# Decode values on column tiles with a norm per sequence, and every channel tile of the convolution as Toeplitz products on 32x32 array tiles

## The chip, the core and the metric

The kernel runs on one core of one Trainium2 chip. The metric is the device time of one execution in microseconds; the time before is 1244.36 us (median of three runs, 1243.08 to 1247.17).

Engines are named as in the profile: PE is TensorE's matmul side and PEld its weight loads, DVE is VectorE, ACT ScalarE, POOL GpSimd, SP the engine that issues most of the DMAs (POOL issues the others).

## The reference

One inference step through two layers, for a prompt of 1024 frames and for 8 running sequences of 16 new frames (1152 tokens together, width 1024). Everything is float32. What matters for the change, shortened:

```python
# layer 0, a running sequence: 1024 cached keys and values and 16 new ones, 4 heads, two maps c
s = einsum('bqhcd,bkhcd->bhcqk', q, k) * 64 ** -0.5 + bias
p = softmax(s)
w = p[:, :, 0] - lam * p[:, :, 1]
o = einsum('bhqk,bkhe->bqhe', w, v)
o = rmsnorm(o, subln_g) * 0.8                    # over the 128 values of a head
out_a = o * silu(g_a)

# layer 1: gated input, depthwise convolution of width 31 over time, LayerNorm over channels
a, b, g = split(rmsnorm(x) @ w_in1, 3)
u = a * sigmoid(b)
ctx = concat([conv_state, u])                    # 30 earlier rows (zeros for the prompt)
c = depthwise_conv(ctx, w_dw) + b_dw             # 1024 channels, each with its own 31 taps
c = silu(layernorm(c)) * silu(g)
y = x + c @ w_out1
```

## The kernel before

Four stages follow each other on the core: the projections of layer 0, the prompt's attention and gating, decode together with layer 0's output projection, and layer 1. Most products are split by hand into a high and a low part in the type fp32r and done as three products (mm3, L155: high times high, low times high, high times low). split_w loads a weight block into one of three raw buffers, ACT casts the high part (L143) and DVE subtracts for the low one (L144). Plain F32 products are also used; the profile shows each of these as two matmul instructions.

The framework orders each engine's instructions by its own estimate of their times and by priorities; each engine then works through its list in order. A DMA waits in the list of the engine that issues it, and what stands behind it waits too.

**Decode.** For each of the 8 sequences, dscores makes scores of 32 rows per head (two maps of 16 queries), the four heads on four column tiles of the array (L730, tiles KT and S), and their exponentials ex. dweights folds the two maps with the matrix cf into transposed weights of 64 columns (4 heads of 16) for 9 key tiles: 8 of the cache and one of the new tokens (L758), and writes them as high and low parts into wt (L761, L762). dvalues loads V in four chunks of 512 KB through two buffers (vraw, L772, issued by POOL), splits each on ACT and DVE (vh L775, vl L776), and makes, for each of the 9 key tiles, two products over all 512 columns (L783, L784, and L784, L786 for the new tokens' tile vs). Only the blocks where a query's head meets that head's columns are wanted, so DVE multiplies by a mask (om, L788), and one F32 product with a placing matrix (L790) puts the 16 rows in their place among 128, where DVE adds them up in oacc (L794). After the last sequence dfinish takes the norms of all sequences and multiplies by the gate. Between these stand prep and main, the output projection of the prompt's token tiles, whose weights are loaded in the first two sequences.

**Layer 1.** conv_tile runs once for each of 8 channel tiles: six groups of 24 products (L155), two for each of three token chunks (b, then a), the sigmoid on ACT (sb, L1103), and u as their product on DVE. Five of the tiles (0, 1, 3, 5, 7) are convolved on DVE by 31 taps for the prompt (L1148, 1024 columns) and 31 for the sequences (L1146). Three (PE_TILES = 2, 4, 6) are convolved on PE: u goes to DRAM (s_u) and comes back as X, with 16 channels by 8 time steps on the partitions; POOL builds block matrices tw from the turned filters (L1166); 5 F32 products of 128x128 for each of 8 groups sum to the result (L1172); ACT copies it to Y (L1173); it goes to DRAM (s_c) and comes back as yb, and ACT adds the bias into cT (L1180, L1183). The four steps of a Toeplitz tile stand behind the third to sixth product groups of the next channel tile (hooks TOEP). msum (L952, POOL) adds up the channel tiles for the LayerNorm. Then come 24 groups of gate products with their SiLU on ACT (sg, L1021), three norm_chunk calls behind gate tiles 4, 5 and 6, and the last projection, whose first weights are loaded after the gates. Products and gates of layer 1 share a PSUM pool (pm2) of three buffers.

## Time and profile before

| | us |
|---|---|
| median of three runs | 1244.36 |
| the profiled execution | 1244.07 |
| its span, first to last instruction | 1242.3 |
| PE busy in the span | 1163.6 |
| DVE busy in the span | 807.9 |
| decode's first scores | 512.25 |
| layer 1's first products | 755.5 |
| the last gate products | 1128 |

The mean granted clock of the span is 0.975. Times within the span count from its start. A PE instruction's duration reaches from its start to its modelled end, and neighbours overlap: what a product costs in a dense row is the distance to the next one's start.

### The profile page before, as it was taken

What the parts mean: (1) busy time and instruction counts of PE and PEld (TensorE: products, weight loads), DVE (VectorE), ACT (ScalarE), POOL (GpSimd) and SP (SyncE); (2) the same over time, 40 slices, a digit from 0 to 9 for tenths busy, and PEclk for the clock granted to TensorE, in tenths of its full rate; (3) what the DMA queues carried; (4) which work ended last, traced back from release to release, by engine and by line L of the source; (5) the groups of instructions that cost most, each with busy time, mean ns of one, the idle gap of its engine ahead of it and who ended that gap; (6) DMA issues with size and microseconds to landing.
All of it is one profiled execution on the core that took longest, in us unless ns stands there. A gap on an engine that the chain in (4) does not pass through costs nothing.

```text
span 1242.3 us, 18215 instructions
## 1 busy us (share of the span) xinstructions
PE 1163.6 (94%) x6516; PEld 1038.4 (84%) x6516; DVE 807.9 (65%) x1663; ACT 461.0 (37%) x1058; POOL 364.3 (29%) x516
## 2 busy tenths in 40 slices
PE   6999999999989997779999998999999987998997
PEld 4878998999989987557776767999999987997886
DVE  5420225688787778765555444899989999267843
ACT  4431223545454545554435334111121212256421
POOL 2232223344354335322322220112424220033300
PEclk9999999999989998889999999999999998999999
DMA  8352444414141314877766646113321310212231
GB/s 298 107 157 73 148 145 136 126 55 120 41 122 46 103 49 137 287 246 238 238 220 237 194 145 174 45 41 89 97 85 60 112 60 24 68 35 102 80 124 68
DMA packets 122042, 153.23 MB, mean 123 GB/s; under 512 B 13697, under 2 KB 85401, under 8 KB 121944
## 3 DMA queue, kind: packets, MB, share of 16 engines
q1 hardware_dynamic: 107968, 108.21, 28.1%
q0 software_dynamic: 13840, 43.60, 10.5%
q8 instruction: 52, 0.85, 0.3%
q14 instruction: 38, 0.31, 0.1%
q10 hardware_dynamic: 144, 0.26, 0.1%
HBM read 116.22 MB, written 36.26 MB: 123 GB/s over the span
## 4 chain that ended last, share of the span: by engine, by line
PE 75%; DMA 9%; DVE 6%; issue 5%; ACT 3%; POOL 1%; SPq 0%; DVEq 0%; POOLq 0%; ACTq 0%
PE mm L155 51%; PE out L155 7%; PE py L1172 3%; PE pa L587 2%; PE tr L416 2%; DMA vraw<-in_cache_v 1%; PE tr L165 1%; PE S L544 1%; PE mm L784 1%; PE S L545 1%; PE mm L783 1%; PE tr L582 1%; DMA big<-s_c 1%; DMA s_c<-big 1%; PE S L730 1%
## 5 line engine op out<-in xcount | busy, mean ns | idle before, releaser
L155 PE MATMUL mm<-yh,wh 128*128 128x384 f32 x576 | 196.4, 341 | 15.2 <-ACT sg L1021 12.7
L155 PE MATMUL mm<-yh,wl 128*128 128x384 f32 x576 | 195.4, 340 | 0.2 <-DVE wl L144 0.2
L155 PE MATMUL mm<-yl,wh 128*128 128x384 f32 x576 | 195.4, 339 | 0.0
L155 PE MATMUL mm<-wh,xh 128*128 128x384 f32 (+1 forms) x504 | 185.4, 369 | 1.5 <-DVE sg L467 0.6
L1148 DVE SCALAR_TENSOR_TENSOR acc<-u,cc,acc 128x1024 f32<-128x1024 f32 x145 | 185.7, 1281 | 0.4
L155 PE MATMUL mm<-wl,xh 128*128 128x384 f32 (+1 forms) x504 | 184.3, 366 | 1.5 <-DVE wl L144 1.5
L155 PE MATMUL mm<-wh,xl 128*128 128x384 f32 (+1 forms) x504 | 183.5, 364 | 0.0
L144 DVE TENSOR_TENSOR wl<-raw,wh 128x1024 fp32r<-128x1024 f32 (+1 forms) x72 | 91.3, 1275 | 91.8 <-ACT wh L143 88.4
L155 PEld LDWEIGHTS mm<-yh,wh 128*128 128x128 f32 x576 | 109.2, 190 | 16.0 <-ACT sg L1021 13.0
L155 PEld LDWEIGHTS mm<-yh,wl 128*128 128x128 f32 x576 | 109.1, 190 | 0.6 <-DVE wl L144 0.5
L155 PEld LDWEIGHTS mm<-yl,wh 128*128 128x128 f32 x576 | 109.2, 190 | 0.3
L155 PEld LDWEIGHTS mm<-wh,xh 128*128 128x128 f32 x504 | 95.7, 190 | 13.1 <-issue 1.1
L155 PEld LDWEIGHTS mm<-wl,xh 128*128 128x128 f32 x504 | 95.6, 190 | 11.4 <-DVE wl L144 2.9
L155 PEld LDWEIGHTS mm<-wh,xl 128*128 128x128 f32 x504 | 95.5, 189 | 8.8 <-DVE xl L168 0.3
L143 ACT CAST wh<-raw 128x1024 fp32r<-128x1024 f32 (+1 forms) x72 | 71.4, 1001 | 70.0 <-PE mm L155 32.2
L124 POOL TENSOR_TENSOR rr<-pw,mhalf 128x1 f32<-128x1 f32 x59 | 38.4, 651 | 165.9 <-DVE pw L123 157.4
L558 ACT ACTIVATE e<-S,nm 128x512 f32<-128x512 f32 (+5 forms) x96 | 55.0, 578 | 53.7 <-DVE nm L553 36.2
L155 PE MATMUL out<-wh,ch 128*128 128x512 f32 x144 | 59.9, 416 | 1.7 <-DVE xr L844 1.2
L1166 POOL TENSOR_TENSOR tw<-wx,same 128x640 f32<-128x640 f32 x24 | 37.3, 1558 | 82.3 <-PE py L1172 72.5
L550 DVE TENSOR_REDUCE nm<-S 128x1 f32<-128x512 f32 (+5 forms) x96 | 52.5, 551 | 10.5 <-PE S L545 9.7
L155 PE MATMUL out<-wh,cl 128*128 128x512 f32 x144 | 58.8, 408 | 0.0
L155 PE MATMUL mm<-wl,ch 128*128 128x512 f32 x144 | 56.4, 392 | 2.3 <-DVE wl L144 2.2
(282 smaller groups left out, 2400.0 us busy)
## 6 DMA issues: line engine op xcount, KB each, us to landing
raw<-in_cache_k SPq DMA_DIRECT2D x32, 512.0 KB, 4.4
vraw<-in_cache_v POOLq DMA_DIRECT2D x32, 512.0 KB, 5.4
raw<-in_w_in SPq DMA_DIRECT2D x24, 512.0 KB, 5.1
raw<-in_w_out SPq DMA_DIRECT2D x16, 512.0 KB, 4.6
raw<-in_w_in SPq DMA_DIRECT2D x32, 256.0 KB, 3.4
raw<-in_w_in SPq DMA_DIRECT2D x48, 128.0 KB, 3.1
s_y<-xr POOLq DMA_DIRECT2D x9, 512.0 KB, 4.7
x<-s_y SPq DMA_DIRECT2D x9, 512.0 KB, 4.2
```

Source lines behind the costliest of these rows:

```text
L124: m = nc.gpsimd.tensor_tensor(out, v[:, :w], self.mhalf[:, :w], ALU.pow)
L143: nc.scalar.copy(h[:, :ks * n], raw[:, :ks * n])
L144: (low or nc.vector).tensor_tensor(l[:, :ks * n], raw[:, :ks * n], h[:, :ks * n].bitcast(F32), ALU.subtract)
L155: m = self.nc.tensor.matmul(out, lhsT=x, rhs=y, start=(i == 0), stop=(i == n - 1))
L165: nc.tensor.transpose(ps[:, k * P:(k + 1) * P], src[:, kk * P:(kk + 1) * P], self.ident)
L416: nc.tensor.transpose(ps[:, h * P:(h + 1) * P], src[:, h * P:(h + 1) * P], self.ident)
L550: nc.vector.tensor_reduce(nm[:, j:j + 1], s[:, :n], AX.X, ALU.max, negate=True)
L558: nc.scalar.activation(e[:, j * n:(j + 1) * n], S[j][:, :n], AF.Exp, bias=nv, accum_out=zz[:, j:j + 1])
L587: nc.tensor.matmul(po, lhsT=wT[:, k * P:(k + 1) * P], rhs=hd["v"][:, k, :], start=(k == 0), stop=(k == qb))
L1148: tap = nc.vector.scalar_tensor_tensor(cv[:, :T] if k == CONV - 1 else acc, u[:, k:k + T], w1, acc, ALU.mult, ALU.add)
L1166: nc.gpsimd.tensor_tensor(tw.rearrange("p s (c f) -> p s c f", f=8), wx[:, g, :].rearrange("p (s f) -> p s f", f=8).unsqueeze(2).broadcast ...
L1172: nc.tensor.matmul(py, lhsT=tw[:, 4 - s, :], rhs=X[:, g, s:s + 176], start=(s == 0), stop=(s == 4))
```

## The change

**Decode.** V is no longer split: the products are plain F32. Each of the 9 key tiles gives four products, one per head, with 16 weight columns and the head's 128 value columns, on the four column tiles; the wanted blocks alone come out, in one 128x128 block of PSUM (pvt). Mask, placing product, oacc and the split of wt are gone. The norm, with the gate, is done per sequence, and the rows are stored for sequences 0 to 6 together and for the last one. V has five buffers (VB), and vload fetches it one sequence ahead. The scores and value products are issued with a raised priority (HPS).

**Layer 1.** All eight channel tiles take the Toeplitz path. The products are 32x32: 4 channels by 8 time steps on each of four row strips. A tile has two steps of 80 products, behind the fourth and fifth group of the next channel tile. Four PSUM banks take the results, rotated over the partitions, and the store to s_c undoes the rotation in seven DMAs. The bias is a step of its own (back), on DVE, behind the first product u of the tile after next. The last two of these stand in the first gate tiles, whose sg buffers are now held from the start. norm_chunk stands behind gate tiles 3, 4 and 5, and the first half of the output weights is loaded from gate tile 4 on.

```diff
-PE_TILES = (2, 4, 6)
+HPS = 300
+VB = 5
-TOEP = (2, 3, 4, 5)
+TOEP = (3, 4)
+HPT = 400
-LN_AT = (4, 5, 6)
+LN_AT = (3, 4, 5)
...
+        def vload(b):
+            if b >= NB:
+                return
+            cv = a["cache_v0"][b].rearrange("(t p) h e -> p t (h e)", p=P)
+            seqs[b]["V"] = []
+            for i in range(4):
+                vr = vp.tile([P, 1024], F32, name="vraw", bufs=VB).rearrange("p (t c) -> p t c", t=2)
+                nc.gpsimd.dma_start(out=vr, in_=cv[:, 2 * i:2 * i + 2])
+                seqs[b]["V"] += [vr[:, 0], vr[:, 1]]
+            seqs[b]["V"].append(vs)
...
         def dvalues(b):
+            wt, V = seqs[b]["wt"], seqs[b]["V"]
+            pav = pvt[:, b % 2 * P:(b % 2 + 1) * P]
+            with tc.high_priority(offset=HPS):
+                for k in range(8, -1, -1):
+                    for h in range(H):
+                        nc.tensor.matmul(pav[h * 32:h * 32 + NQ], lhsT=wt[:, k, h * NQ:(h + 1) * NQ],
+                                         rhs=V[k][:, h * P:(h + 1) * P], start=(k == 8), stop=(k == 0))
             jk = ep.tile([P, P], F32, name="jk", bufs=1)
+            ss = self.small.tile([P, 1], F32, name="ss")
+            nc.scalar.activation(jk, pav, AF.Square, accum_out=ss)
+            rm = self.small.tile([P, 1], F32, name="rr")
             self.rpow(rm, ss, 1.0 / P, 1e-6)
+            nc.vector.scalar_tensor_tensor(og[:, b], pav, rm, gs[:, b], ALU.mult, ALU.mult)
...
             if b > 0:
                 dvalues(b - 1)
+                vload(b)
...
         dvalues(NB - 1)
         prep(6)
-        dfinish()
...
+            for i in range(8):
...
+                late = (lambda j=i - 2: back(j)) if i > 1 else None
+                tiles.append(self.conv_tile(i, wb, pm, ub, cT[i], chan, (s_u, s_c), same, hooks_of(i), late))
...
+            if c == 0 and late is not None:
+                with tc.issue_after(mu.ins if hasattr(mu, "ins") else mu):
+                    late()
...
         def step(q):
+            tw = ub.tile([P, 20, 32], F32, name="tw", bufs=2)
+            nc.gpsimd.tensor_tensor(
+                tw.rearrange("p s (c f) -> p s c f", f=8),
+                wx[:, 4 * q:4 * q + 4].rearrange("p g (s f) -> p (g s) f", f=8).unsqueeze(2).broadcast_to([P, 20, 4, 8]),
+                same.rearrange("p (c f) -> p c f", f=8).unsqueeze(1).broadcast_to([P, 20, 4, 8]), ALU.mult)
+            with tc.high_priority(offset=HPT):
                 for s in range(5):
+                    for j in range(4):
+                        for r in range(4):
+                            rs, c = slice(r * 32, (r + 1) * 32), (r + j) % 4
+                            nc.tensor.matmul(self.py[j][c * 32:(c + 1) * 32, q * 256:q * 256 + 176],
+                                             lhsT=tw[rs, j * 5 + 4 - s, :], rhs=X[rs, 4 * q + j, s:s + 176],
+                                             start=(s == 0), stop=(s == 4))
+            for j in range(4):
+                nc.scalar.copy(Y[:, 4 * q + j, :], self.py[j][:, q * 256:q * 256 + 176])
+            if q == 0:
+                return
+            sv = s_c[i].rearrange("(g p) m -> p g m", p=P)
+            for j in range(4):
+                k = j * 32
+                nc.sync.dma_start(out=sv[:P - k, j::4], in_=Y[k:, j::4])
+                if j:
+                    nc.sync.dma_start(out=sv[P - k:, j::4], in_=Y[:k, j::4])
+            yb = ub.tile([P, 8, 176], F32, name="big", bufs=4)
+            nc.sync.dma_start(out=yb, in_=s_c[i].rearrange("(p f) m -> p f m", f=8))
...
+        def back():
+            yb, bia = ret["yb"], chan[:, i, 0:1]
+            nc.vector.tensor_scalar(cv[:, :T].rearrange("p (m f) -> p m f", f=8),
+                                    yb[:, :, :P].rearrange("p f m -> p m f"), bia, None, ALU.add)
```

Three places in the built order show what moved. Rows give the line, the operation and output<-inputs with the output's rows and columns; a count at the end joins like rows. The changed program's line numbers are its own.

PE at the first value products of decode, before:

```order
L758 MATMUL mm<-cf,ex 128x64 x9
L416 MATMUL tr<-cst_58,raw 128x128 x8
L783 MATMUL mm<-vh,wt 128x512
L784 MATMUL mm<-vl,wt 64x512
L783 MATMUL mm<-vh,wt 128x512
L784 MATMUL mm<-vl,wt 64x512
```

and now, at the same place (L759 is the weights, L414 the key transposes, L782 the values, pv the new PSUM block):

```order
L759 MATMUL mm<-cf,ex 128x64 x8
L759 MATMUL pv<-cf,ex 128x64
L414 MATMUL tr<-cst_58,raw 128x128 x8
L782 MATMUL pv<-vs,wt 16x128 x4
L782 MATMUL pv<-vraw,wt 16x128 x32
```

The 18 products over 512 columns became 36 products of 16x128, which read V as it was loaded and stand in one piece.

PE at the first Toeplitz step of a channel tile, now (py_8250 to py_8253 are the four banks; the row behind is a projection). Before, a step had two rows of five products with 128 rows, L1172, with projections between them:

```order
L1140 MATMUL py_8250<-big,tw 32x176 x4
L1140 MATMUL py_8251<-big,tw 32x176 x4
L1140 MATMUL py_8252<-big,tw 32x176 x4
L1140 MATMUL py_8253<-big,tw 32x176 x4
L1140 MATMUL py_8250<-big,tw 32x176 x4
```

Each row of four holds the four row strips of one bank, and the sixteen products of four rows share no array tile; five such blocks are a step.

ACT at the first gate, before (L1173 copies Toeplitz results, L1180 and L1183 add the bias, L1021 is the gates' SiLU):

```order
L1173 COPY big<-py 128x176 x2
L1180 ACTIVATE cT_8260<-big,cc 128x1024
L1183 ACTIVATE cT_8260<-big,cc 128x8x8 x2
L1021 ACT_TABLE_LOAD
L1021 ACTIVATE sg_10366<-mm 128x384 x3
```

and now (L1144 copies Toeplitz results, L146 casts weights, L958 is the SiLU):

```order
L1144 COPY big<-py_8253 128x176
L146 CAST wh<-raw 128x1024 x2
L958 ACT_TABLE_LOAD
L958 ACTIVATE sg_8268<-mm 128x384 x2
```

No addition of a bias stands ahead of the first SiLU any more; it is on DVE.

More of the change, by code (lines that the diff above doesn't have):

```diff
@@ L796, in dfinish @@
-        def dfinish():
-            ss = self.small.tile([P, H], F32, name="ss4")
+            wt = ep.tile([P, 9, 64], F32, name="wt", bufs=2)
+            ps = pm.tile([P, 512], F32, name="mm")
+            p8 = pvt[:, 256 + b % 2 * 64:320 + b % 2 * 64]
+            for k in range(9):
+                nc.tensor.matmul(ps[:, k * 64:(k + 1) * 64] if k < 8 else p8, lhsT=ex[:, k, :], rhs=cf,
+                                 start=True, stop=True)
+            nc.scalar.copy(wt[:, :8], ps.rearrange("p (k e) -> p k e", e=64))
@@ new lines, in phase_conv @@
+            chan = cp.tile([P, 8, 4], F32, name="cc")
+            same = cp.tile([P, 32], F32, name="same")
+            nc.sync.dma_start(out=chan, in_=self.s_cc.rearrange("p (i n) -> p i n", n=4))
+            nc.sync.dma_start(out=same, in_=a["cst"][:, C_SAME:C_SAME + 32])
+            s_u = self.dram.tile([8, P * 8, 180], F32, name="s_u")
+            s_c = self.dram.tile([8, P * 8, 176], F32, name="s_c")
+            s3 = E(ExitStack())
+            ubs = ExitStack()
+            ub = ubs.enter_context(tc.tile_pool(name="ub", bufs=2, reuse_waits="tile"))
@@ new lines, in phase_conv, with back, hooks_of @@
+            tiles = []
+            def back(i):
+                tiles[i][2]()
+                if i == 1:
+                    nc.gpsimd.tensor_tensor(msum, cT[0], cT[1], ALU.add)
+                elif 1 < i < 7:
+                    nc.gpsimd.tensor_tensor(msum, msum, cT[i], ALU.add)
+            def hooks_of(i):
+                hooks = {}
+                if i > 0:
+                    hooks[TAIL] = [tiles[i - 1][0]]
+                    for p, f in zip(TOEP, tiles[i - 1][1]):
+                        hooks.setdefault(p, []).append(f)
+                return hooks
@@ L969, in phase_conv @@
+            for i in range(2):
+                if i == 0:
+                    wb = self.split_w(wp, [a["w_in1"][:, 2 * D:2 * D + 256]], 256)
+                gate_tile(i, wb)
+                if i == 0:
+                    back(6)
+            back(7)
+            ubs.close()
             pl.close()
@@ L1091, in hook @@
             nonlocal npc
-            with self.tc.issue_after(m):
+            with tc.issue_after(m):
                 for f in hooks.get(npc, ()):
@@ L1189 @@
+        return tail, [lambda q=q: step(q) for q in range(2)], back
 _INS = ["x_prompt", "x_sample", "cache_k0", "cache_v0", "state_conv1", "rel_bias", "norm_g0", "w_in0",
```

290 lines of the change are left out of this document (87 added, 203 removed).

## The prediction

> **What bounds the kernel now.** I read the page's busy shares, its slices and its chain first.
>
> ```profile
> PE 1163.6 (94%) x6516; PEld 1038.4 (84%) x6516; DVE 807.9 (65%) x1663; ACT 461.0 (37%) x1058; POOL 364.3 (29%) x516
> ...
> PE   6999999999989997779999998999999987998997
> ...
> DVE  5420225688787778765555444899989999267843
> ...
> PE 75%; DMA 9%; DVE 6%; issue 5%; ACT 3%; POOL 1%; SPq 0%; DVEq 0%; POOLq 0%; ACTq 0%
> ```
>
> TensorE is busy nearly everywhere and carries 75% of the chain. VectorE is full only in slices 25 to 34, the convolution. So work taken from VectorE is worth only what TensorE waits for it, and work taken from TensorE counts where nothing else sets the pace. The stages differ, so I cut the span into decode, convolution with gates, and the last projection; columns are the stretch, then busy us and count for PE, weight loads, DVE, ACT, POOL, then granted clock, DMA share, GB/s.
>
> ```profile
> 512.25:755.50 243.25, 224.06 (x1305) 166.19 (x1304) 131.88 (x221) 107.75 (x207) 65.56 (x88) 0.96 0.66 219
> 755.50:1128.00 372.50, 352.88 (x2060) 348.73 (x2059) 305.67 (x421) 91.79 (x169) 91.76 (x84) 0.98 0.24 73
> 1128.00:1242.30 114.30, 103.53 (x455) 83.70 (x453) 69.45 (x160) 44.89 (x125) 20.72 (x16) 0.98 0.27 97
> ```
>
> The change touches the first two rows: 616 us. A PE busy time includes the tail of each product, so below I use the distance between starts instead.
>
> **Decode values.** The old value products, three groups of the lines view, and single rows of the timeline:
>
> ```profile
> L783 PE MATMUL mm<-vh,wt 128*128 128x512 f32 x64 | 28.2, 440 | 5.2 <-DVE wt L762 5.2
> L790 PE MATMUL mm<-om,mk 128*128 128x512 f32 x16 | 8.3, 598 | 0.0
> ...
> 706.08 0.40 PE L783 MATMUL mm<-vh,wt 128*128 128x512 f32 x1
> 706.31 0.40 PE L784 MATMUL mm<-vl,wt 128*64 128x512 f32 x1
> ...
> 512.25 1.50 PE L730 MATMUL S<-KT,qz 128*32 128x256 f32 x24
> ...
> 684.10 0.39 PE L783 MATMUL mm<-vh,wt 128*128 128x512 f32 x1
> 684.42 0.67 PE L730 MATMUL S<-KTx,qz 128*32 128x272 f32 x8
> 685.01 0.44 PE L165 MATMUL tr<-cst,raw 128*128 128x128 f32 x2
> ```
>
> A sequence has 9 key tiles, each with a high and a low product: 18 starts 0.23 us apart (706.08, 706.31) are 4.1 us, and the placing product adds 8.3/8 = 1.0. Eight sequences: 41 us. The new products have not run, but their like has: L730 puts the four heads on four column tiles. An F32 product is two passes, so its 24 instructions are 6 groups of four; 1.50 us less one product's 0.38 (the rest of a tail) leaves 5 steps of 0.22 us. Four of 256 columns thus cost what one would: the column tiles do run side by side. With 128 columns a group costs 0.11, and 9 tiles in two passes make 18 groups: 2.0 us. Entering and leaving the tiling costs about 0.1 us each way (684.10 to 684.42 is 0.32 where 0.23 is usual; 684.42 to 685.01 is 0.59 for two groups of 0.25). So 2.2 us a sequence, 17.6 in all: TensorE is relieved of 23.8 us. ACT's and DVE's splits of V go as well; they matter only through the next rows.
>
> How much arrives? The chain of waits inside decode, with start and length of its pieces, and two windows:
>
> ```profile
> 646.07 5.49 PE out L155 x24
> ...
> 657.04 2.59 DVE vl L776
> ...
> 659.92 8.15 DMA vraw<-in_cache_v
> ...
> 699.02 6.08 PE out L155 x19
> ...
> 540.00:550.00 10.00, 8.59 (x69) 5.69 (x67) 8.33 (x12) 6.14 (x9) 3.73 (x5) 1.00 1.00 355
> 600.00:627.00 27.00, 27.00 (x169) 19.97 (x169) 15.26 (x26) 12.59 (x25) 8.98 (x13) 1.00 0.76 233
> ```
>
> The same piece returns after two sequences, so a period is 52.95/2 = 26.5 us. It goes through the V load: a load (8.15) starts only once the low split has freed one of two buffers (657.04). The new five buffers, filled a sequence ahead, cut that link. What is late next is TensorE or the DMA engines: they move 6.3 MB a period at a share of 0.76, and 26.5 less 2.8 would put them at 0.85, below the 1.00 and 355 GB/s that they reach elsewhere. In the first two sequences the loads of keys, V and output weights set the pace (share 1.00 in 540 to 550), so there I count nothing. I take six periods of 2.8: **-17 us**. Ends: 0 (the loads take it all) and -41 (all 23.8, and some 2 us a period of present waiting as well).
>
> **The wait ahead of the gates.** PE and ACT rows of the timeline; brackets give the wait and who ended it.
>
> ```profile
> 1018.58 0.33 PE L155 MATMUL mm<-yl,wh 128*128 128x384 f32 x1
> 1018.75 0.34 PE L155 MATMUL mm<-yh,wl 128*128 128x384 f32 x1
> 1018.93 1.68 PE L1172 MATMUL py<-big,tw 128*128 128x176 f32 x10
> 1033.32 0.69 PE L155 MATMUL mm<-yh,wh 128*128 128x384 f32 x1 [12.71 <-ACT sg L1021]
> 1033.80 0.52 PE L155 MATMUL mm<-yl,wh 128*128 128x384 f32 x1
> 1034.12 0.52 PE L155 MATMUL mm<-yh,wl 128*128 128x384 f32 x1
> ...
> 1028.84 2.03 ACT L1180 ACTIVATE cT<-big,cc 128x1024 f32<-128x1024 f32 x1 [7.90 <-DMA big<-s_c]
> ```
>
> ACT stands at L1180, the bias of the last Toeplitz tile, until its DMA round trip lands; the first gate's SiLU is queued behind it, and TensorE has no PSUM buffer left. It then starts cold: 0.32 us apart for 0.17, some ten products, 1.5 us. The new code gives this bias to DVE (back) and issues gate products in between, so ACT has no round trip ahead of the SiLU: **-14.2**. If DVE or the release of the old pool's memory took its place, 0.
>
> **Toeplitz products.** The rows of the convolution window:
>
> ```profile
> L1148 DVE SCALAR_TENSOR_TENSOR acc<-u,cc,acc 128x1024 f32<-128x1024 f32 x145 | 185.7, 1281 | 0.4
> ...
> L1172 PE MATMUL py<-big,tw 128*128 128x176 f32 x240 | 40.1, 314 | 3.0 <-DMA big<-s_u 3.0
> ```
>
> The 185.7 us of taps, with their companions, leave VectorE and are worth nothing by themselves: beside them stand TensorE's projections. Old Toeplitz: ten instructions in 1.68 us less a 0.31 tail are 0.149 each (1.37/9 is 0.152), so 240 cost 35.8 us for three channel tiles. New: eight tiles of two steps, a step 80 products of 32x32, 160 instructions. If all sixteen array tiles run at once that is 10 waves of 0.15, plus 0.2 for changing the tiling, plus 0.2 for a wave not quite closed: 1.9 us, 30.4 for 16 steps. **-5.4**. Bounds from the nearest rows: sixteen at once 1.7 a step; four at once, which is all that L730 shows, 160/4 x 0.149 + 0.2 = 6.2 a step, 99 in all. I take the near end because four tiles lost nothing against one, and the order of the 80 gives sixteen neighbours each a tile of its own. The Trainium skill, "TensorE: Matmul & The Clock Gate", "Measured speedup vs the span model", has 10.6 times for 16 tiles; by that figure, an estimate, a step is 2.45 us, 39 in all, and the total 9 us higher. No run here shows it yet.
>
> The 3.0 us of waiting for big<-s_u goes too: the steps stand after the fourth and fifth of six groups, no longer from the third: **-3.0**.
>
> **The return path.** The added waits: back waits on DVE for the yb load, with the next product u behind it; POOL's msum add waits for back, the next tw builds behind that, and TensorE for tw.
>
> ```profile
> L1173 ACT COPY big<-py 128x176 f32<-128x176 f32 x24 | 7.4, 306 | 81.9 <-PE py L1172 81.9
> L1166 POOL TENSOR_TENSOR tw<-wx,same 128x640 f32<-128x640 f32 x24 | 37.3, 1558 | 82.3 <-PE py L1172 72.5 <-issue 7.5 <-ACT sb L1103 2.3
> L952 POOL TENSOR_TENSOR msum<-msum,cT 128x1152 f32<-128x1152 f32 x5 | 13.3, 2664 | 31.8 <-ACT cT L1183 28.2 <-DVE cT L1148 3.6
> ...
> 898.57 0.81 SPq L1069 DMA_DIRECT2D sn<-in_state_conv  x2
> ...
> s_u<-big SPq DMA_DIRECT2D x3, 720.0 KB, 3.8
> big<-s_u SPq DMA_DIRECT2D x3, 720.0 KB, 4.6
> s_c<-big SPq DMA_DIRECT2D x3, 704.0 KB, 3.7
> big<-s_c SPq DMA_DIRECT2D x3, 704.0 KB, 4.1
> ```
>
> A group is 24 x 0.173 = 4.2 us, a tile 6 groups and two steps: 29 us. The second step ends at 25.0; four copies of 0.31 to 26.3; seven writes at 0.41 and 3.7 to land, 33; yb 4.1 more, 37, which is 8 us into the next tile. Back is due behind the first product u at 9.2, so it just doesn't wait. Its own DVE cost is not in the trace: ACT's form took 2.03, so 2.6 with the two small ones; then msum 2.7 and tw 1.6 end at 16.1, and the step needs it at 16.8. On SP, s_u goes behind yb at 4.6, lands at 8.4, and X at 13.0. So all covers hold, by 0.7 us on POOL: I add **+2** for the tiles where it doesn't, between 0 and 24 (4 us in six tiles).
>
> **The rest.** The first output weights load a gate earlier, and LayerNorm starts a gate earlier:
>
> ```profile
> L155 PE MATMUL mm<-wl,ch 128*128 128x512 f32 x144 | 56.4, 392 | 2.3 <-DVE wl L144 2.2
> ```
>
> The 2.3 us at most: **-2.3**. The per-sequence norms, the eight turned filters in the setup and the constants lie beside TensorE in their stages: 0, a microsecond either way.
>
> **Sum.** 1244.1 (the profiled execution; the median of three is 1244.4) -17 -14.2 -5.4 -3.0 +2 -2.3 = **1204**.
>
> **Rivals.**
>
> *Fewer tiles at once: slower.* The sixteen tiles of a wave put four row strips in one PSUM bank, and no row of the trace has row strips at all. The gains and the new Toeplitz time make 39.9 + 30.4 = 70.3 us; over 16 steps that is 4.4 us, so below 160 x 0.149/4.2 = 5.7 tiles at once the kernel is slower than before. At four it gives 1204 + 69 = **1273**. For it: only column tiles are seen side by side. Against it: those share a bank and lose nothing. The Trainium skill's "TensorEngine Tiling (Array Packing)", "Gotcha 1: PSUM Pressure", says that different row tiles cannot use one bank at the same time; by that rule this is the outcome, and the trace cannot say.
>
> *Eight at once.* The two F32 passes of a product go to the same array tile; if only four neighbours are interleaved, half the array waits: 160/8 x 0.149 + 0.2 = 3.2 a step, 51 in all: **1225**.
>
> *Decode is bound by its loads.* The V and key bytes stay: **1221**.
>
> *The return path is late* by 3 us in six tiles: **1220**. SP's seven writes in place of one speak for it, the timetable above against it.
>
> **How the numbers follow.** Forecast 0.62; slower by too few tiles 0.12; eight at once 0.09; loads 0.09; return path 0.08. The range takes the middle rivals in and, below, most of the waits in decode: 1186 to 1236. Left out are the slower case and some 6% below. This kernel's runs tell 0.3% (3.7 us) from no change. All cases but one are faster by more; I leave 0.03 for gains and losses that cancel: faster 0.85, same 0.03, slower 0.12.
>
> **What would show it.** Right: a step of 80 products lasting about 1.9 us; sequences under 24.5 us apart in decode; no wait above 3 us between the last step and the gates; DVE busy for about a third of its time of before in the convolution. Wrong: steps above 3 us, TensorE waiting for tw or big<-s_u in every tile, DMA share near 1 throughout decode, or a wait for a SiLU at the third gate.

## The result, and the profile after

The changed kernel takes 1261.59 us (median of 4 runs, 1258.58 to 1265.88); the kernel before, on the same chip, 1245.76 us. The ratio is 1.0133, 95% interval 1.0102 to 1.0163: slower by 1.3%, where 1204 us was predicted. The profiled execution took 1258.6 us, its span 1256.8, 14.5 more than the 1242.3 of before. Of all executions here one was disturbed, the profiled one of decode_kr3_gs below (2892.53 us); it is left out, so that kernel has no trace.

The windows view of the changed kernel, cut where the three stages of before were cut (first score product, first product of layer 1's projections, end of the gate products; columns as in the prediction):

```profile
521.20:762.40 241.20, 203.00 (x1721) 161.47 (x1721) 81.84 (x176) 77.91 (x175) 62.10 (x91) 0.93 0.63 217
762.40:1144.20 381.80, 366.38 (x4385) 346.44 (x4384) 103.80 (x157) 99.32 (x216) 95.45 (x91) 0.99 0.38 112
1144.20:1256.80 112.60, 102.18 (x447) 83.76 (x446) 56.03 (x137) 37.22 (x109) 8.87 (x12) 0.96 0.28 98
```

The work went where the change sends it: in decode TensorE's busy time falls from 224.06 to 203.00 us, in the second stage VectorE's from 305.67 to 103.80. The stages did not follow. Decode starts 9.0 us later (521.20 for 512.25) and is 2.0 us shorter; convolution and gates are 9.3 us longer; the last projection is 1.7 us shorter. Together that is the 14.5 us.

**Where decode went.** Pieces of the timeline in a steady sequence (start, length, engine; brackets give the wait and what ended it). SP and POOL issue loads, PE is TensorE:

```profile
632.72 2.90 POOL L772 DMA_DIRECT2D vraw<-in_cache_v  x4 [5.37 <-PE pv L782]
...
635.72 5.95 SPq L696 DMA_DIRECT2D raw<-in_cache_k  x3
...
638.72 0.67 PE L732 MATMUL S<-KTx,qz 128*32 128x272 f32 x8 [0.33 <-ACT KTx L415]
...
641.34 0.40 PE L158 MATMUL out<-wl,ch 128*128 128x512 f32 x1
644.90 1.09 PE L414 MATMUL tr<-cst,raw 128*128 128x128 f32 x4 [3.16 <-DMA raw<-in_cache_k]
645.64 0.78 PE L158 MATMUL out<-wh,cl 128*128 128x512 f32 x1
...
647.07 0.63 PE L158 MATMUL out<-wh,cl 128*128 128x512 f32 x1
647.50 0.63 PE L158 MATMUL out<-wh,ch 128*128 128x512 f32 x1
...
651.62 0.40 PE L158 MATMUL out<-wh,ch 128*128 128x512 f32 x1
651.85 0.39 PE L158 MATMUL out<-wl,ch 128*128 128x512 f32 x1
...
668.37 0.67 PE L732 MATMUL S<-KTx,qz 128*32 128x272 f32 x8 [0.33 <-ACT KTx L415]
```

The value products of a sequence now run in one piece and free V's buffers together, so POOL issues four V loads, 2 MB, at 632.7 to 635.6. The first key load of the next sequence goes out at 635.72, behind them. SP could not send it earlier: it waited for one of the three shared buffers, which the key transposes at 634.7 to 635.7 gave free, and these stand behind the value products. The keys are there at 644.90, 9.2 us after the issue, and TensorE has waited 3.2 us for them. Then it runs at half clock (the granted clock is 0.50 from 645.0 to 650.5, 1.00 behind): output products 0.43 us apart (647.07, 647.50) where 0.23 is usual (651.62, 651.85), twelve of them. So one late load costs some 6 us, and the period, from scores to scores, is 668.37 - 638.72 = 29.6 us; before it was 26.5, and 23.7 was forecast. (The next period is 29.5, the two ahead took 23.0 and 25.4, so the stage as a whole still got 2.0 shorter.) The DMA share of the stage is 0.63, so over the stage the engines have room. But between 636 and 645 us, while this load is under way, the share is 0.98 to 0.99: the load stands behind a burst that fills the engines.

**Where the start went.** The same view ahead of decode:

```profile
487.75 2.94 POOL L772 DMA_DIRECT2D vraw<-in_cache_v  x4
...
489.18 2.00 SPq L667 DMA_DIRECT2D gs<-s_ga  x4
491.23 8.96 SPq L672 DMA_DIRECT2D bs<-s_rel  x7
501.54 0.56 SPq L673 DMA_DIRECT2D qs<-s_qh  x1
...
502.87 1.08 SPq L696 DMA_DIRECT2D raw<-in_cache_k  x2
...
509.17 1.94 PE L414 MATMUL tr<-cst,raw 128*128 128x128 f32 x8 [7.85 <-DMA raw<-in_cache_k]
```

Two key loads of sequence 0 went out long before (422 and 432 us; in the old kernel 421 and 436); what follows is the third, called the first key load below. Five buffers let POOL prefetch V at once (a fifth load follows at 492.2). Behind those loads SP's small ones are slow; it takes 9 us for seven loads of bs and reaches the key load at 502.87. In the old kernel it went out 11 us earlier:

```profile
491.65 0.41 SPq L696 DMA_DIRECT2D raw<-in_cache_k  x1
```

**Where the convolution went.** The way of the last tile's samples, the Toeplitz steps, and (second fence: who waited, for whom, us in all, times, longest) TensorE's waits from the last tile on:

```profile
1022.57 1.23 DVE L1159 TENSOR_SCALAR cT<-big,cc 128x1024 f32<-128x1024 f32 x1 [5.30 <-DMA big<-s_c]
...
1024.09 0.65 DVE L1098 TENSOR_TENSOR big<-mm,sb 128x256 f32<-128x256 f32 x1
...
1024.32 2.67 POOL L934 TENSOR_TENSOR msum<-msum,cT 128x1152 f32<-128x1152 f32 x1 [9.74 <-DVE cT L1162]
1026.93 1.44 POOL L1105 COPY big<-utmp 128x128 f32<-128x128 f32 x1
...
1028.52 0.47 SPq L1123 DMA_DIRECT2D s_u<-big  x1
1034.68 0.37 SPq L1125 DMA_DIRECT2D big<-s_u  x1
...
812.02 2.65 PE L1140 MATMUL py<-big,tw 32*32 32x176 f32 x153
815.54 0.50 PE L1140 MATMUL py<-big,tw 32*32 32x176 f32 x7 [0.86 <-issue]
815.97 0.45 PE L158 MATMUL mm<-yh,wh 128*128 128x384 f32 x1
...
844.48 2.72 PE L1140 MATMUL py<-big,tw 32*32 32x176 f32 x160
847.13 0.44 PE L158 MATMUL mm<-yh,wh 128*128 128x384 f32 x1
...
1039.36 4.26 PE L1140 MATMUL py<-big,tw 32*32 32x176 f32 x160 [5.30 <-DMA big<-s_u]
1043.55 0.44 PE L158 MATMUL mm<-yh,wh 128*128 128x384 f32 x1
```

```profile
PE py L1140 <- DMA big<-s_u: 5.3, 1, 5.3
PE ln L1001 <- POOL ac L997: 2.7, 2, 1.4
...
PE mm L158 <- DVE wl L147: 1.5, 2, 0.7
PE mm L158 <- ACT sg L958: 1.2, 1, 1.2
PE ln L1002 <- POOL ac L997: 0.9, 2, 0.6
```

A step takes 847.13 - 844.48 = 2.65 us, not 1.9. Three of the sixteen pause inside for over a microsecond (812.02: 3.95 us to the next product), and the last tile's first step starts at half clock after a wait of 5.3 us (4.19 us). From first product to the next product after, the sixteen sum to 47.9 us. The 24 groups of before, measured in the same way (the last one without the 12.71 us behind it), sum to 33.4. The old wait of 12.71 us for ACT is gone, as forecast, with 3.0 us for big<-s_u. In their place stand the 5.3 us, and 6.3 us from there to 1150 us (3.7 of them up to the last gate product), more than half of it for POOL's sums of squares in norm_chunk. The 5.3 us begin on VectorE: it stands for 5.30 us at back (L1159) of the tile before, whose return load is under way, and the last product u (L1098) is queued behind. They go on at POOL: since back is done first, its sum msum (L934) stands ahead of the copy of u's last columns (L1105), which ends at 1028.4 where u was ready at 1024.9. So U is stored at 1028.52, read back from 1034.68, and the step that was due at 1034.1 starts at 1039.36.

### The profile page after: what moved, and what is told of

It is laid out like the page before. It is cut to its first block, busy times and chain, and to the rows that moved or that the text cites. A ratio compares the mean times of both kernels' runs of the same rounds, so it can differ in the third digit from the quotient of the medians.

```text
span 1256.8 us, 23483 instructions
## 1 busy us (share of the span) xinstructions
PE 1157.8 (92%) x9254; PEld 1034.5 (82%) x9254; DVE 540.5 (43%) x1332; ACT 429.5 (34%) x1055; POOL 355.9 (28%) x525
## 5 line engine op out<-in xcount | busy, mean ns | idle before, releaser
L147 DVE TENSOR_TENSOR wl<-raw,wh 128x1024 fp32r<-128x1024 f32 (+1 forms) x72 | 87.7, 1228 | 205.8 <-ACT wh L146 204.3
L146 ACT CAST wh<-raw 128x1024 fp32r<-128x1024 f32 (+1 forms) x72 | 71.8, 1003 | 70.3 <-PE mm L158 29.9
L414 PE MATMUL tr<-cst,raw 128*128 128x128 f32 x260 | 42.4, 304 | 29.1 <-DMA raw<-in_cache_k 23.8
L414 PEld LDWEIGHTS tr<-cst,raw 128*128 128x128 f32 x260 | 33.7, 157 | 36.5 <-issue 25.4
L1098 DVE TENSOR_TENSOR big<-mm,sb 128x384 f32<-128x384 f32 (+1 forms) x24 | 20.2, 840 | 94.7 <-PE mm L158 68.0
L158 PE MATMUL out<-wl,ch 128*128 128x512 f32 x144 | 58.2, 404 | 0.0
```

Source lines behind the costliest of these rows:

```text
L146: nc.scalar.copy(h[:, :ks * n], raw[:, :ks * n])
L147: (low or nc.vector).tensor_tensor(l[:, :ks * n], raw[:, :ks * n], h[:, :ks * n].bitcast(F32), ALU.subtract)
L158: m = self.nc.tensor.matmul(out, lhsT=x, rhs=y, start=(i == 0), stop=(i == n - 1))
L414: nc.tensor.transpose(ps[:, h * P:(h + 1) * P], src[:, h * P:(h + 1) * P], self.ident)
L1098: mu = nc.vector.tensor_tensor(dst, pa_[:, :n].rearrange("p (m f) -> p m f", f=8), sb[:, :n].rearrange("p (m f) -> p m f", f=8), ALU.mult)
```

## The experiments

Start times of products cut each trace into the same five pieces: from the last product of the input projections to the first score; to the first product of layer 1; to the last Toeplitz product; to the last high-times-high product of the gates; to the end of the span. Us, one profiled execution each:

| kernel | to scores | decode | conv | gates | last | span |
|---|---|---|---|---|---|---|
| before | 28.5 | 243.5 | 264.5 | 107.5 | 114.5 | 1242.3 |
| changed | 35.2 | 241.2 | 287.9 | 93.2 | 113.3 | 1256.8 |
| decode_only | 31.4 | 243.7 | 273.5 | 107.9 | 115.5 | 1253.9 |
| conv_only | 25.8 | 250.0 | 284.5 | 93.1 | 114.6 | 1253.3 |
| late_gs | 32.4 | 239.4 | 282.9 | 92.8 | 115.0 | 1248.7 |
| kr3 | 31.4 | 218.3 | 283.4 | 90.7 | 116.8 | 1226.5 |
| before_kr3 | 33.0 | 235.5 | 267.4 | 108.0 | 115.0 | 1243.4 |
| decode_kr3 | 36.1 | 211.1 | 276.1 | 107.9 | 115.3 | 1228.8 |
| hps0 | 35.2 | 224.2 | 281.4 | 93.0 | 113.1 | 1230.9 |
| kr3_ln456 | 30.3 | 218.9 | 283.8 | 84.8 | 115.0 | 1217.5 |
| best | 33.7 | 212.8 | 282.5 | 84.8 | 114.8 | 1213.2 |
| best_hps0 | 34.4 | 207.3 | 288.0 | 84.8 | 115.0 | 1213.9 |

### Each half alone

The decode half (buffers, order, column tiles, norms, loads) in front of the old convolution, and the new convolution behind the old decode.

> The decode half of the change (score and value order with priority, values on column tiles, five buffers for V, norms of each sequence) in front of the convolution of before. Theory A, the loss has two halves: the decode stage is itself 7 us longer than before (from 501 us to the first product of the convolution it took 254.5 us before and 261.4 us after), so this kernel is 4 to 10 us slower than before, near 1252 us. Theory B, the whole loss is the convolution's: the decode part gains the 17 us that were forecast as soon as the old convolution stands behind it, near 1228 us. Theory C, the decode part is neutral by itself and only its late start carries into the stages behind it: within 3 us of before.

> The convolution half of the change (all eight channel tiles as Toeplitz products on 32x32 array tiles) behind the decode of before. Theory A: the convolution and gates stage is about 10 us longer than before (steps 47.9 us in place of 35.8 us, a wait of 5.5 us for the last tile's samples, about 8 us of waits among the gates, against 16 us of waits that are gone), so 6 to 12 us slower than before, near 1254 us. Theory B, the convolution half gains and the decode half loses all: near 1225 us. Under A the two halves add up to the change within 4 us.

decode_only: 1257.47 us, ratio 1.0101 (1.0085 to 1.0118). conv_only: 1252.88 us, ratio 1.0067 (1.0042 to 1.0093). Both halves lose by themselves, 12 and 8 us, and the whole loses 16. A gain of one half that the other eats is ruled out. But much of either loss lies in a stage whose code is the old one. Of the 11.6 us of decode_only's span, 9.0 are in the old convolution, where TensorE waits 8.0 us for big<-s_u (3.0 before); its decode, with the start, is only 3.1 longer, so Theory A had the place wrong. Of conv_only's 11.0 us, 5.6 are in its convolution and gates, and the old decode takes 6.5 longer. Why the unchanged stages got longer was not tried.

### The start of decode

```diff
 def setup():
     nc.sync.dma_start(out=fold, ...)
-    nc.gpsimd.memset(gs, 0.0)
-    for h in range(H):
-        nc.sync.dma_start(out=gs[...], in_=self.s_ga[...])
-    nc.sync.dma_start(out=vs, in_=self.v0s)
...
+def setup2():
+    ...    # the lines taken out of setup
...
-return [setup] + [lambda i=i: keys_part(0, (i,)) for i in range(4)]
+return [setup] + [lambda i=i: keys_part(0, (i,)) for i in range(4)] + [setup2]
```

> The changed kernel with one part of the change moved: the four loads of the gates' values and the load of the new values into the decode buffers are issued behind the keys of sequence 0, not ahead of them. Theory A (the small loads fill the ring of outstanding loads of SP and wait behind 2.6 MB of V loads, so the first key load is issued 11 us late): the first key load goes out 6 to 11 us earlier against the rest of the stage, the wait of 8 us ahead of the first key transpose shrinks to under 4 us, and the kernel is 5 to 9 us faster than the changed one, near 1254 us. Theory B (the V loads alone make the first keys late, wherever the small loads stand): the first key transpose waits as long as now and the time stays within 3 us of 1261 us.

1250.76 us, ratio 1.0049 (1.0028 to 1.0071): 11 us faster than the changed kernel, a little more than Theory A had it. The first key load goes out 10.2 us earlier:

```profile
492.66 1.29 SPq L698 DMA_DIRECT2D raw<-in_cache_k  x1
494.04 3.15 SPq L680 DMA_DIRECT2D gs<-s_ga  x3
```

So the small loads did hold back the keys. But the first scores come only 2.8 us earlier, since a wait of 5.7 us for DVE takes the place of the one for keys, and TensorE then waits 7.8 us for ACT between the first two score groups. Of the 8.1 us by which the span is shorter, the table places 2.8 at the start, 1.8 in decode and 5.0 in the convolution. The edit doesn't touch that code, but the program's order on VectorE there is another:

```profile
1014.58 0.68 DVE L1100 TENSOR_TENSOR big<-mm,sb 128x256 f32<-128x256 f32 x1
...
1020.54 1.22 DVE L1161 TENSOR_SCALAR cT<-big,cc 128x1024 f32<-128x1024 f32 x1 [5.13 <-DMA big<-s_c]
```

Here the last product u stands ahead of back, and the last tile's step doesn't wait. The start is thus worth 3 to 5 us; the other 5 go with the order of VectorE and POOL at the last tile, which changes with the schedule as a whole. All of back is ahead of u, and POOL's sum ahead of its copy, in the changed kernel, conv_only, last45 and best_hps0; the three of them whose step stands in the old slot wait 5.3, 5.5 and 5.0 us. In kr3 and kr3_ln456 only back's long instruction is ahead, POOL copies at once, and the step waits 0.7 and 0.9 us. In late_gs, kr3_gs, kr3_order, hps0, best and best_last back is behind, and it waits 0.6 us at most. This was read from the traces; no experiment changed that order alone.

### The wait for keys: buffers

```diff
-kr = self.rawp.tile([P, 1024], F32, name="raw")...
+kr = ktp.tile([P, 1024], F32, name="kraw", bufs=3)...
```

> The changed kernel with a key buffer of its own: the key loads of decode rotate through three buffers that nothing else uses, and the three buffers of before stay for weights and rows. Theory A (TensorE waits 3.3 to 4.2 us in each steady sequence for a key load that could not start until a batch of transposes released its buffer, and then runs some 5 us at half clock): the waits for keys between 610 and 700 us go below 1 us each, the period falls from 29.6 us to about 24 us in the sequences that show it, and the kernel is 12 to 25 us faster than the changed one, 1237 to 1250 us. Theory B (the DMA engines are the limit and the loads only queue longer): the DMA share in decode is near 0.8, the waits stay, and the time is within 4 us of 1261 us.

> The kernel of before with three key buffers of its own in decode, nothing else. Theory A (the shared buffers limit the changed kernel only, since its transposes stand in batches; before, the period of 26.5 us goes through the two V buffers and the V split): the period stays at 25.5 to 26.5 us and the time is within 5 us of before, 1240 to 1247 us; the decode half of the change is then worth about 14 us or more once keys have their own buffers. Theory B (the shared key buffers bounded before as well): the period falls to 24 us or less and the time to 1220 to 1232 us, as far as the changed kernel's fell, and the decode half of the change is worth next to nothing.

> The decode half of the change with three key buffers of its own, in front of the convolution of before. Theory A (the two halves add up: the convolution half costs 7.7 us by itself, and the changed kernel with key buffers took 1226.5): near 1219 us, 1214 to 1223, with the period at 23.0 us. Against the kernel of before with the same key buffers (1242.4) the decode half is then worth about 23 us, close to the 23.8 us by which TensorE is relieved. Theory B (the new convolution needs less of DVE, ACT and the DMA engines while decode ends, so the halves help each other): 1226 us or more.

kr3: 1226.54 us, ratio 0.9857 (0.9834 to 0.9880), 35 us less than the changed kernel, more than Theory A had it, and faster than before. Of the 30.3 us in the spans the table places 26.7 at the start and in decode; 4.5 are in the convolution, where the last tile's wait is gone. The period is 23.0 us in each of the four steady sequences (two score groups below), and between 560 and 730 us TensorE has no wait for keys.

```profile
624.99 0.67 PE L732 MATMUL S<-KTx,qz 128*32 128x272 f32 x8 [0.67 <-POOL rr L127]
...
647.99 0.67 PE L732 MATMUL S<-KTx,qz 128*32 128x272 f32 x8 [0.67 <-POOL rr L127]
```

The windows of the changed kernel, then of kr3, over the same 100 us:

```profile
600.00:700.00 100.00, 86.13 (x799) 68.86 (x799) 30.49 (x74) 29.70 (x70) 31.17 (x46) 0.95 0.65 220
```

```profile
600.00:700.00 100.00, 95.26 (x862) 77.02 (x863) 34.22 (x83) 34.36 (x85) 33.25 (x46) 1.00 0.69 241
```

A higher DMA share with fewer waits: over a period the engines were not the limit. The burst is still there (share 0.97 to 1.00 from 646 to 660 us), and key loads behind V take 10.7 and 11.1 us (issued at 645.47 and 646.80). With buffers of their own they are sent early enough that nobody waits. before_kr3: 1242.41 us, ratio 0.9969 (0.9948 to 0.9991); the period stays at 26.4, so the old kernel was not bound by these buffers, and Theory A holds. decode_kr3: 1233.00 us, ratio 0.9909 (0.9876 to 0.9943). There Theory A failed in its sum, 1219, and the time is the one that Theory B names, though no run shows B's reason. The decode pieces came out as it said (36.1 + 211.1 = 247.2 us against 268.5 in before_kr3: 21.3 us gained), but the old convolution got longer, 276.1 us for 264.5 in before. In it TensorE waited 8.2 us for big<-s_u, where before it waited 3.0. As in decode_only, the cause of that was not tried.

### The wait for keys: order

```diff
-HPS = 300
+HPS = 0
```

> The changed kernel without the priority for the score and value products (offset 0 in place of 300); buffers as in the change. Theory A (the order makes the waits: sixteen key transposes in a row release all buffers at once): transposes and value products alternate again, the waits for keys in the steady sequences fall below 1 us and the time falls to 1235 to 1250 us. Theory B (three buffers shared by keys, weights and rows are too few for the shorter period whatever the order): the waits stay, 1255 to 1270 us.

1233.54 us, ratio 0.9907 (0.9879 to 0.9935): 28 us faster than the changed kernel, by one number, with the shared buffers. Of the 25.9 us in the spans 17.0 are in decode and 6.5 in the convolution, where the last tile's order is the other one. The timeline of hps0 in a steady sequence:

```profile
651.88 2.62 SPq L696 DMA_DIRECT2D raw<-in_cache_k  x2
...
653.39 0.74 POOL L772 DMA_DIRECT2D vraw<-in_cache_v  x1
...
657.67 0.66 PE L168 MATMUL tr<-cst,raw 128*128 128x128 f32 x4
658.16 0.60 PE L414 MATMUL tr<-cst,raw 128*128 128x128 f32 x4
```

Key transposes now stand ahead of and between the value products, so a key load goes out first (651.88) and lands 4.0 us later, the V loads follow one by one (653.39 to 657.3), and the transposes at 658.16 don't wait. Theory A holds in its cause: the time is below its range, though some waits for keys stay (3.2 us between 600 and 700, the longest 2.2, where it said below 1).

> As best (key buffers of its own, small loads behind the first keys, norm pieces one gate later), and without the priority for score and value products. Theory A (one wait, the key load that lands late behind the V loads; either edit hides it): within 3 us of best, 1215 to 1221 us, the steady period 23 us in both. Theory B (two waits): at least 8 us faster than best, 1210 us or less.

1220.46 us against 1217.56 for best (ratios 0.9795, 0.9771 to 0.9819, and 0.9780): no difference in the time. Neither kernel waits for keys between 600 and 700 us, so order and buffers are two cures of that wait. But the equal times hide two differences: the steady period is 22.1 us, not 23, and decode 5.5 us shorter (table), and the convolution is 5.5 longer, with 5.0 us of waiting at the last tile.

### The Toeplitz steps

First the products of the shifts s > 0 on 88 columns, which leaves out part of the convolution; then the loops over row strip and bank exchanged. Both on kr3.

```diff
+m = 88 if s else 176
-nc.tensor.matmul(self.py[j][..., q * 256:q * 256 + 176], lhsT=..., rhs=X[rs, 4 * q + j, s:s + 176],
+nc.tensor.matmul(self.py[j][..., q * 256:q * 256 + m], lhsT=..., rhs=X[rs, 4 * q + j, s:s + m],
...
-for j in range(4):
-    for r in range(4):
+for r in range(4):
+    for j in range(4):
```

> The changed kernel with three key buffers of its own, and the Toeplitz products of the four later shifts on 88 of their 176 columns (that part of the convolution is left out). Theory A (a step is bound by the pace at which TensorE takes instructions, 160 weight loads and products at 16.6 ns each): a step still takes 2.6 to 2.7 us. Theory B (bound by the columns that stream through each array tile, 10 instructions of 0.265 us): a step takes 0.53 + 4 x 0.27 = 1.6 us.

> The changed kernel with three key buffers of its own, and the Toeplitz products in another order: the four products that follow each other share a row strip and write to four banks, where now four that follow each other lie in four row strips and write to one bank. Theory A (pace of the instructions): a step stays within 0.1 us of 2.65 us. Theory B (four row strips that write to one bank at the same time get in each other's way): a step falls towards the 1.5 us to 1.9 us that sixteen tiles at once give at the rate of the 128x128 products of before.

The timelines of kr3_half, then of kr3_order:

```profile
815.84 2.14 PE L1141 MATMUL py<-big,tw 32*32 32x176 f32 x160
817.91 0.44 PE L158 MATMUL mm<-yh,wh 128*128 128x384 f32 x1
```

```profile
820.29 2.72 PE L1140 MATMUL py<-big,tw 32*32 32x176 f32 x160
822.95 0.45 PE L158 MATMUL mm<-yh,wh 128*128 128x384 f32 x1
```

kr3_half: 2.07 us a step, between the two theories (2.65 and 1.6). Four shifts shrank by 0.145 us each; half the columns of two passes at the old rate are 2 x 88 x 0.149/176 = 0.149 us. So all sixteen tiles do run at once (with eight, half the columns would have saved twice as much): a shift is two passes of 0.149 us, as forecast, plus 0.23 us (2.65/5 - 0.298) that does not shrink with the columns. The starts in the trace fit that: instructions mostly start 16 to 17 ns apart, so the sixteen tiles of a shift start over some 0.25 us. That this is the whole of the 0.23 us was not tried. kr3_order: 2.66 us, as before, and 1228.43 us in one run. With sixteen tiles at once four row strips are at work in each bank in either order, so it is the step's time, not this run, that answers the rival of four tiles: 2.65 us where four at once would take 6.2. Four row strips that write to one bank at the same time, each to its own 32 partitions, cost nothing that can be seen here.

### The last tile and the norms

```diff
-for f in hooks_of(8).get(3 * i + c, ()):
+for f in hooks_of(8, (4, 5)).get(3 * i + c, ()):
...
-LN_AT = (3, 4, 5)
+LN_AT = (4, 5, 6)
...
-if i == LN_AT[1]:
+if i == 4:
```

The first pair is last45, on the changed kernel: the last tile's steps stand at slots 4 and 5 in place of 3 and 4. The others are kr3_ln456, on kr3; the load of the output weights keeps its place.

> The changed kernel with the two Toeplitz steps of the last channel tile one slot (24 products, 4.2 us) later among the gates. Theory A (TensorE waits 5.3 us in front of the last tile's first step for the samples that come back from memory, and runs at half clock behind the wait, while products of the gates that depend on nothing stand behind it): the wait falls below 1.5 us and the kernel is 4 to 8 us faster than the changed one, near 1255 us. Theory B (the path back of the last tile then ends later by the same 4.2 us and the norms wait for it in its place): within 2 us of 1261 us.

> The changed kernel with key buffers of its own and the three norm pieces one gate later, where the kernel of before has them (the load of the output weights stays where the change put it). Theory A (TensorE waits 4 to 8 us among the gates for the sums of squares on POOL, since the pieces follow too closely on the last tile's return): the waits for POOL's sums fall below 1 us in all and the time falls by 3 to 6 us to 1220 to 1224 us. Theory B (the last piece then ends inside the last projection, whose first products wait for it): the waits move there and the time is within 2 us of 1226.5 us.

last45: 1258.01 us, ratio 1.0108 (1.0082 to 1.0134), not to be told from the changed kernel. The wait falls from 5.3 to 1.0 us, but those for POOL's sums rise from 3.6 to 5.9 us: half of it moved to the norms, as Theory B has it. kr3_ln456: 1218.36 us, ratio 0.9783 (0.9762 to 0.9804), 8 us less than kr3. In kr3 TensorE waits 5.7 us for POOL's sums, here not at all. The gates shrink from 90.7 to 84.8 us, the last piece from 116.8 to 115.0: the norm pieces stood one gate too early.

### Together

> The changed kernel with key buffers of its own and the small loads of gate values and new values moved behind the keys of sequence 0. Theory A (two causes, two prices: the late first keys cost about 11 us whatever buffers the keys have): first key load before 493 us in place of 498.8, 1216 to 1221 us. Theory B (with free buffers the three key loads go out together and overtake what was lost; the stage's start is then bound by the DMA engines, whose share there is 0.84): within 3 us of 1226.5 us.

> The decode half of the change with key buffers of its own and the small loads behind the keys of sequence 0, in front of the convolution of before. Theory A (all terms add): 1206 to 1213 us, the fastest of all, near the 1204 us that were forecast though by another road. Theory B (the start of decode is bound by the DMA engines once keys have their buffers): as decode_kr3, near 1219 us.

> The changed kernel with all three repairs: three key buffers of its own, the small loads behind the keys of sequence 0, the norm pieces one gate later. Theory A (three separate causes): 1226.5 less 4.7 (small loads) less 8.2 (norm pieces) gives 1213 to 1215 us. Theory B (one cause seen three times, a wait that only moves): 1218 us or more.

> As best, with the two steps of the last tile one slot (24 products) later among the gates. Theory A (the last tile's wait of about 1 us in front of its first step is all that is left of it): 1 to 2 us faster than best. Theory B (the return path of the last tile becomes late for the norms by 4 us): the same or slower than best.

kr3_gs: 1221.81 us, ratio 0.9807 (0.9789 to 0.9825), between its two theories; the first key load goes out at 490.71. decode_kr3_gs: 1235.57 us, ratio 0.9912 (0.9897 to 0.9927), nothing gained on decode_kr3 and far above both theories. best: 1217.56 us, ratio **0.9780** (0.9757 to 0.9803), 27 us faster than before and the fastest of all with kr3_ln456; it lies between its theories, so the small loads added less than the sum said. best_last: 1219.01 us, ratio 0.9790 (0.9765 to 0.9815), the same. So keys and norms add up; the start of decode, worth 11 us on the changed kernel (5 of them in the convolution) and 5 on kr3, adds no more than 1 behind kr3_ln456.

## Why the prediction was wrong

Term by term, in its own order.

- **Decode values, -17: wrong. Of it -2.0 arrived in the stage, with +6.7 ahead of it.** The relief was there: TensorE's busy time fell by 21 us for a forecast of 23.8, and with key buffers the period is 23.0 us, and 21 us arrive (decode_kr3 against before_kr3). What failed is the step "what is late next is TensorE or the DMA engines". It looked at the V chain alone and at the share of the DMA engines. The key loads rotate through three buffers that they share with weights and rows, and the new priority put 2 MB of V ahead of them. The rival "decode is bound by its loads" named the place, but took the bytes for the cause. The share was 0.63 over the stage, full only in the burst, and one number in the order took most of the wait away. The start of decode is 9.0 us later, of which 6.7 lie behind the input projections; the 2.3 ahead of that are within the spread of the traces here (481.9 to 486.2 us).
- **"The per-sequence norms ... beside TensorE: 0" and "there I count nothing" for the first sequences: wrong.** The norms brought four loads onto SP's queue ahead of the first keys, and five buffers for V brought 2.5 MB ahead of both. Every instruction that a moved step issues was to be counted; these were not.
- **The wait ahead of the gates, -14.2: right.** No wait for a SiLU at the third gate. That a wait takes its place was weighed only for DVE and for the old pool's memory. It came from the return path instead, below.
- **Toeplitz, -5.4: a size was off.** Sixteen tiles at once held; the term that was too small is "0.2 for a wave not quite closed": it was counted once a step and measures 0.23 us in each of five shifts. With 2.65 us a step the sixteen come to 42.4 us, not 30.4, and with the pauses (last section) and the cold step to 47.9, against 33.4 by the same measure for the old groups (35.8 in the prediction): +14.5. The rivals of four and of eight tiles are ruled out by kr3_half. The estimate of 2.45 us from the Trainium skill ("TensorE: Matmul & The Clock Gate", "Measured speedup vs the span model") was nearer than 1.9.
- **Waits for big<-s_u, -3.0: right for seven tiles**, and 5.3 us for the eighth.
- **The return path, +2: the mechanism right, the place and size off.** "back waits on DVE for the yb load, with the next product u behind it" happened with effect for one tile, the last, and cost 5.3 us and 1.5 for the cold step. POOL's sum, which the prediction had holding up the next tw, held up the copy of u in its place. The seven tiles before were covered. For the last one the schedule put back ahead of the third product u, behind which it stands in the code; the timetable of the prediction had looked at the first. TensorE never waits for tw.
- **Output weights and norms a gate earlier, -2.3: wrong.** The last stage gained 1.2 to 1.7 us, but the norms stood before their sums were ready; a gate later gave 8 us on kr3.

For convolution and gates the measured terms are +14.5 (steps), -14.2 and -3.0 (old waits), +5.3 and +3.7 (new waits up to the last gate product): +6.3 of the 9.3 us. The rest was not traced.

In sum: the two large gains, -17 and -14.2, were real as mechanisms. They were spent on Toeplitz steps that cost more than the old groups, where a gain was forecast, and on waits that the change itself had made: in the queue of loads, in the order of VectorE and POOL at the last tile, and in the order of the gates.

## What to carry to other kernels

When an engine is relieved, list every load of the stage with its buffers and the queue it stands in, not only those that the old chain ran through: an average DMA share of 0.63 says nothing about a load that stands behind 2 MB of others. Raising the priority of one kind of product also moves the moment when its buffers come free, and so the place of its loads among all others; here that was worth 17 us in decode. And a late load costs more than its wait, since TensorE came back at half clock (granted clock 0.50) both times: 3.2 us of waiting cost some 6, and 5.3 cost 6.8.

## What the runs showed of the hardware

Three of the sixteen Toeplitz steps pause for 1.0 to 1.4 us in the middle, in the changed kernel, kr3, kr3_order and last45 alike. Counted in TensorE's program order (weight loads, products and recorded waits), the pauses stand behind instructions 9921, 12736 and 15552: 2815 and 2816 apart, eleven times 256. The trace has 73 packets of 16 KB on an instruction queue, one for each 256 of TensorE's 18,763 recorded instructions. In each step that pauses such a packet starts 0.9 to 1.2 us after the step's begin, and the pause ends 1.2 to 1.5 us after it has landed. In kr3_half (one packet starts at 1.6) the steps run faster, the pauses stand behind the same three instructions and are longer (1.5 to 1.9 us), and they end as late after the step's begin (3.3 to 3.8 us). conv_only, where the blocks of 256 fall elsewhere, has none over 0.3 us. So the pauses look like waits for code: a step issues 320 instructions in 2.65 us, more than a block, and where one boundary falls near its start, the next comes before the code has. The Trainium skill, "Runtime: NRT & Kernel Launch", "Instruction fetch mechanics", states blocks of 16 KiB, 256 instructions, and the cost of crossing one as mostly hidden; the size agrees, the hiding does not hold for these steps of 32x32 products. The pauses cost 3.6 us in the changed kernel. Their cause was read from the traces and not tried by an experiment of its own.
